# Half-swap copies of the second mixer: issued from GpSimd's queue in place of SyncE's

## Chip, cores and metric

One core of one Trainium2 chip runs the whole program. The metric is the time in microseconds (us) of one execution on the device, as the median of the timed runs. "us" and "ns" below are taken from timed runs and from one profiled execution. PE is TensorE's matmul unit, DVE VectorE, ACT ScalarE, POOL GpSimd and SP SyncE; "SPq" is the row of the instructions with which SP starts transfers.

## What is computed

The reference is a trunk of two layers over 512 positions of width 1024. Each layer has a mixer, a cross-attention into 256 memory tokens and a gated feed-forward part with a short convolution. The second layer's mixer is the one that matters here:

```
def mixer_cd(hn, w_in, w_out, ...):
    u_c, h_d = split_sizes(hn @ w_in, (C_WIDTH, 2 * D_WIDTH))
    y_f = s5_scan(u, ...)                       # a complex diagonal recurrence over the 512 positions
    y_b = flip(s5_scan(flip(u), ...))           # the same, backwards
    y = y_f + y_b + d_skip * u_c
    z = gelu(y);  o_c = z * sigmoid(z @ w_glu + b_glu)
    o_d = conformer_conv(h_d, ...)              # gate, 31-tap depthwise convolution, layernorm, silu
    return concatenate([o_c, o_d]) @ w_out
```

## The kernel before

Activations are held with channels on the 128 partitions and the 512 positions along the free dimension. Every large matmul is done three times over float32r operands that are split into a high and a low part: `wload` copies a 128x1024 block of weights to `wh` on ACT (line 201) and subtracts it to get `wl` on DVE (line 202), and `mm3` issues the three products (lines 206, 207, 208). The raw weights come from HBM into three rotating buffers `wr`, all by SP (line 147), in one fixed order; a load can start when the `wl` subtraction of three loads earlier has freed its buffer.

The second mixer runs four groups of 128 channels (i = 0 to 3). The string `CD` writes out the order of its stages; a letter and the group name each. The stages that matter:

- `c` and `C` (`c_`, lines 1365 to 1389) are the forward and the backward scan of a group. PE makes the scan's input (line 1374), ACT copies it to `t1` (tile name T, line 1377), and two transfers of 64 partitions each write `t1s` as `t1` with its upper and lower halves swapped (lines 1378 and 1379): real and imaginary parts sit on the two halves. DVE then multiplies `t1` in place by a table (line 1380), multiplies `t1s` (1381), adds (1382), scans (1384 or 1386), and multiplies the scan's result twice (1387, 1388). Line 1380 overwrites `t1`, so it waits for both transfers.
- `s` (`s_`, lines 1391 to 1396) swaps the halves of both results of a group into `xs` (tile X2s), again by two transfers for each direction; they wait for line 1388.
- `x` (line 1402) adds on DVE what `s` brought to what line 1387 left; `y` (lines 1416 and 1418) multiplies the sum on PE.
- `q` is two of the 31 taps of the convolution, each one instruction on DVE (line 1463); 'u', 'v' and 'g' are blocks of the input projection, 'k' steps of the keys and values of the next cross-attention, 'w' and 'Z' load and apply convolution tables for PE.
- `l`, `L`, `m` load tables for the scans (tiles bm, cst, cm) from scratch in HBM, all by SP. The tile cst has two buffers: the load for a group waits until line 1388 of the group before has read its old contents.

So SP's queue holds three kinds of work in one order: half-swap copies, table loads and weight loads. SP waits for the inputs of the instruction at its head before it goes on. A planner orders each engine's instructions by its own estimate of when they can run; `pinned` fixes, for the engines that it is given, that the first instruction of a stage stays behind the last one traced before it. In this mixer these are PE and SP (`PS_`, line 1536), DVE for `q`. GpSimd's only use of its own queue for transfers is line 793, in the first mixer, which loads four tiles of the input (256 KB each, 128 partitions).

Of the kernel before, what the change touches and what calls it, by code (L numbers as in the profile page):

```python
# [90 lines left out]
def trunk(ctx, tc, xT, memT, pos, vec, amask, cmask, bmask,  # L91
          w_z, w_ab, w_abv, w_oab, w_xq, w_xk, w_xv, w_xo, w_up, w_dn, wg2,
          w_cd, w_glu, w_ocd, s5v, s5b, s5bs, s5c, s5cs, ctab, out, upto=99):
    nc = tc.nc
    V, A, G, PE = nc.vector, nc.scalar, nc.gpsimd, nc.tensor
# [7 lines left out]
    def nm(p):  # L103
        n_[0] += 1
        return f"{p}_{n_[0]}"
# [32 lines left out]
    def tp_ps():  # L138
        return PS.tile([128, 512], F32, tag="tp", bufs=2, name=nm("tp"))
# [1118 lines left out]
    def mixer_cd(norm, nnext, kv):  # L1258
# [3 lines left out]
        def b2(tag, bufs):  # L1262
            return T.tile([128, S], F32, tag=tag, bufs=bufs, name=nm(tag))
# [20 lines left out]
        def half0(j):  # L1284
            if j in part:
                return
            H, L = wload(None, 1024, wnext(srcs, WAHEAD), G if j in LPOOL else V)
            part[j] = mm_ps(), H, L
            half1(j, 0)
            if j == first:  # L1290
                half1(j)
# [73 lines left out]
        def c_(i, d):  # L1365
            BM, cst = tab[i, d], rot[i, d]
            ct, st, rt = cst[:, 0], cst[:, 1], P.tile([128, S], F32, tag="nsq", bufs=2, name=nm("rt"))
            A.activation(g3(rt), rho[:, 32 * d + 8 * i:32 * d + 8 * i + 8].unsqueeze(2).to_broadcast([128, 8, 64]),
                         AF.Copy)
            V.memset(g3(rt)[:, :, 63 * d:63 * d + 1], 0.0)  # L1370
            fl = (lambda v: g3(v)) if d == 0 else (lambda v: g3(v)[:, :, ::-1])
            tp = tp_ps()
            for g in range(8):
                PE.matmul(tp[:, 64 * g:64 * g + 64], BM[:, 128 * g:128 * g + 128], Rg[i][:, 64 * g:64 * g + 64],
                          start=True, stop=True)
            t1, t1s = b2("T1", 3), b2("T1s", 2)
            A.activation(t1, tp, AF.Copy)
            nc.sync.dma_start(t1s[0:64], t1[64:128])
            nc.sync.dma_start(t1s[64:128], t1[0:64])
            V.tensor_tensor(g3(t1), g3(t1), fl(ct), ALU.mult)  # L1380
            V.tensor_tensor(g3(t1s), g3(t1s), fl(st), ALU.mult)
            V.tensor_tensor(t1, t1, t1s, ALU.add)
            if d == 0:
                V.tensor_tensor_scan(t1s, rt, t1, 0.0, op0=ALU.mult, op1=ALU.add)
            else:
                V.tensor_tensor_scan(t1s[:, ::-1], rt[:, ::-1], t1[:, ::-1], 0.0, op0=ALU.mult, op1=ALU.add)
            V.tensor_tensor(g3(t1), g3(t1s), fl(ct), ALU.mult)
            V.tensor_tensor(g3(t1s), g3(t1s), fl(st), ALU.mult)
            X[i, d] = t1, t1s

        def s_(i):
            for d in range(2):
                xs, t1s = b2("X2s", 2), X[i, d][1]
                nc.sync.dma_start(xs[0:64], t1s[64:128])
                nc.sync.dma_start(xs[64:128], t1s[0:64])
                X[i, d] = X[i, d][0], xs

        def x_(i):
# [130 lines left out]
        def k_(i):  # L1529
            for _ in range(min(i, len(ksteps))):  # L1530
                if ksteps[0] == kv.norm:
# [1 line left out]
                ksteps.pop(0)()  # L1533
                tabset("gelu_apprx_tanh_and_others", True)

        PS_ = (PE, nc.sync)
        stage = {"u": (PS_, u_), "a": (PS_, a_), "b": (PS_, b_), "x": ((), x_), "y": (PS_, y_),
                 "l": (PS_, l_), "L": (PS_, r_), "m": (PS_, m_), "s": (PS_, s_),
                 "c": (PS_, lambda i: c_(i, 0)), "C": (PS_, lambda i: c_(i, 1)),
                 "f": (PS_, f_), "v": (PS_, lambda i: half0(4 + i)), "V": (PS_, v_),  # L1540
                 "g": (PS_, lambda i: half0(8 + i)), "G": (PS_, g_),
                 "A": (PS_, ca_), "B": (PS_, cb_), "w": (PS_, w_), "Z": (PS_, z_), "q": ((V,), q_), "F": (PS_, cf_), "N": (PS_, n_),
                 "k": (PS_, k_), "K": (PS_, lambda i: kv.load())}
# [79 lines left out]
    eskv = ExitStack()  # L1623
    kv1 = KV(1, eskv)
    mixer_cd(n3, n4, kv1)
    if upto == 3:
        return dump()
# [106 lines left out]
```

## Time and profile before

| | us |
|---|---|
| median of 3 runs | 1602.35 |
| lowest and highest | 1599.77, 1603.43 |
| the profiled execution, as timed | 1605.85 |
| its span, first to last instruction | 1604.1 |
| PE busy in the span | 1558.4 (97%) |
| DVE, ACT, POOL busy | 1072.0, 707.6, 327.3 |

The second mixer's scans lie between about 884 and 1008 us of the span. A row of the timeline gives start, duration, engine, line, tiles and, in brackets, how long the engine was idle just before and what ended that. A row of SPq is the issue of a transfer, not the transfer. In a table of stretches each engine's busy time stands with its count of instructions, then the granted TensorE clock as a share of 2.4 GHz, the DMA engines' busy share and the rate in GB/s.

### The profile page before, as it was taken

The page shows a single profiled execution, that of the slowest core. Times are in us where ns is not written, and L with a number is a line of the kernel's source. Part 1 is how long each engine was busy: PE and PEld are TensorE (multiplying, and loading weights), DVE is VectorE, ACT ScalarE, POOL GpSimd, SP SyncE. Part 2 cuts the span into 40 slices and gives each one's busy share as a digit, 9 for nine tenths or more (in the row PEclk, how much of TensorE's full clock was granted, in tenths as well). Part 3 has the DMA queues.
Part 4 walks back from the last instruction along what each step waited for, and adds up shares of the span by engine and source line. Part 5 has one row for each costly group of instructions (what it writes and reads, how often), then busy time and mean ns, then how long its engine had stood idle before and what let it go on. Part 6 is the DMA issues. An engine that isn't in the chain of part 4 may idle for free.

```text
span 1604.1 us, 20956 instructions
## 1 busy us (share of the span) xinstructions
PE 1558.4 (97%) x8036; PEld 1303.9 (81%) x8036; DVE 1072.0 (67%) x1492; ACT 707.6 (44%) x1089; POOL 327.3 (20%) x354
## 2 busy tenths in 40 slices
PE   9999999999999998998999998999999999999997
PEld 6787889888888776786788877888888888888887
DVE  7586766467568789479846797476646766636644
ACT  5464755355444344233336343374535444424423
POOL 8402000000049953553520000000000111100101
PEclk9999999999999999999999999999999999999998
DMA  5323333231222334544545666453202232332331
GB/s 179 109 65 94 110 114 106 79 118 57 76 73 94 120 116 122 168 125 128 149 151 202 210 223 224 157 184 107 90 27 92 94 103 93 96 101 92 95 104 65
DMA packets 76117, 189.11 MB, mean 118 GB/s; under 512 B 8368, under 2 KB 27440, under 8 KB 76016
## 3 DMA queue, kind: packets, MB, share of 16 engines
q1 hardware_dynamic: 75376, 186.58, 36.1%
q8 instruction: 63, 1.03, 0.3%
q0 software_dynamic: 320, 1.05, 0.2%
q14 instruction: 38, 0.31, 0.1%
q10 hardware_dynamic: 320, 0.13, 0.0%
HBM read 162.43 MB, written 19.01 MB: 113 GB/s over the span
## 4 chain that ended last, share of the span: by engine, by line
PE 70%; DVE 13%; POOL 6%; DMA 4%; ACT 3%; issue 3%; SPq 1%; ACTq 0%; DVEq 0%; POOLq 0%
PE mm L206 20%; PE mm L208 20%; PE mm L207 20%; DVE wl L202 2%; PE mm L737 2%; PE sc L1489 1%; DVE t L972 1%; DMA T1s<-T 1%; DVE t L971 1%; PE tp L724 1%; DVE t L976 1%; POOL t L1139 1%; PE sc L208 1%; PE sc L206 1%; PE sc L207 1%
## 5 line engine op out<-in xcount | busy, mean ns | idle before, releaser
L201 ACT ACTIVATE wh<-wr 128x1024 fp32r<-128x1024 f32 (+1 forms) x229 | 239.0, 1045 | 428.4 <-PE mm L207 311.3
L208 PE MATMUL mm<-hg,wl 128*128 128x512 f32 x1000 | 392.9, 393 | 15.9 <-DVE wl L202 15.9
L206 PE MATMUL mm<-hg,wh 128*128 128x512 f32 x1000 | 396.9, 397 | 1.3 <-ACT wh L201 1.3
L207 PE MATMUL mm<-hg,wh 128*128 128x512 f32 x1000 | 391.3, 391 | 0.0
L202 DVE TENSOR_TENSOR wl<-wr,wh 128x1024 fp32r<-128x1024 f32 (+1 forms) x229 | 296.2, 1294 | 76.4 <-ACT wh L201 74.4
L208 PEld LDWEIGHTS mm<-hg,wl 128*128 128x128 f32 x1000 | 189.0, 189 | 60.3 <-DVE wl L202 19.8
L206 PEld LDWEIGHTS mm<-hg,wh 128*128 128x128 f32 x1000 | 189.2, 189 | 42.9 <-issue 2.2
L207 PEld LDWEIGHTS mm<-hg,wh 128*128 128x128 f32 x1000 | 189.1, 189 | 39.5 <-issue 1.2
L976 POOL TENSOR_TENSOR t<-t,t 128x512 f32<-128x512 f32 x22 | 28.9, 1315 | 626.7 <-ACT t L182 622.7
L208 PE MATMUL mm<-g,wl 128*128 128x512 f32 x324 | 126.7, 391 | 2.7 <-DVE wl L202 2.7
L206 PE MATMUL mm<-g,wh 128*128 128x512 f32 x324 | 126.9, 392 | 0.0
L207 PE MATMUL mm<-g,wh 128*128 128x512 f32 x324 | 126.2, 389 | 0.0
L968 DVE TENSOR_TENSOR u<-mm,R 128x512 f32<-128x512 f32 x88 | 60.3, 687 | 74.2 <-PE mm L208 74.0
L970 ACT ACTIVATE t<-u,vt 128x512 f32<-128x512 f32 x88 | 70.8, 806 | 50.3 <-DVE u L968 50.2
L986 DVE TENSOR_TENSOR h<-mm,h 128x512 f32<-128x512 f32 x40 | 27.6, 691 | 87.8 <-PE mm L208 87.7
L972 DVE SCALAR_TENSOR_TENSOR t<-u,vt,t 128x511 f32<-128x511 f32 x88 | 78.5, 892 | 4.3 <-DMA dct<-tr 1.8
L971 DVE SCALAR_TENSOR_TENSOR t<-u,vt,t 128x511 f32<-128x511 f32 x88 | 75.4, 857 | 8.0 <-ACT t L970 8.0
L208 PEld LDWEIGHTS mm<-g,wl 128*128 128x128 f32 x324 | 60.8, 188 | 16.4 <-DVE wl L202 3.5
L182 ACT ACTIVATE t<-t 128x512 f32<-128x512 f32 x44 | 27.8, 633 | 104.2 <-DVE t L972 104.2
L207 PEld LDWEIGHTS mm<-g,wh 128*128 128x128 f32 x324 | 60.8, 188 | 12.6
L206 PEld LDWEIGHTS mm<-g,wh 128*128 128x128 f32 x324 | 60.9, 188 | 12.2
L279 DVE TENSOR_TENSOR h<-mm,h 128x512 f32<-128x512 f32 x32 | 21.7, 688 | 46.2 <-PE mm L208 46.2
(520 smaller groups left out, 2981.7 us busy)
## 6 DMA issues: line engine op xcount, KB each, us to landing
wr<-in_w_up SPq DMA_DIRECT2D x88, 512.0 KB
wr<-in_w_dn SPq DMA_DIRECT2D x32, 448.0 KB
wr<-in_w_ab SPq DMA_DIRECT2D x16, 512.0 KB
wr<-in_w_xv SPq DMA_DIRECT2D x16, 512.0 KB
wr<-in_w_xk SPq DMA_DIRECT2D x16, 512.0 KB
wr<-in_w_xq SPq DMA_DIRECT2D x16, 512.0 KB
wr<-in_w_xo SPq DMA_DIRECT2D x16, 512.0 KB
wr<-in_w_dn SPq DMA_DIRECT2D x16, 512.0 KB
```

What stands on the lines that cost most here:

```text
L182: tabbed(A.activation(dst, src, fn, **kw))
L201: A.activation(H[:, :n], raw[:, :n], AF.Copy)
L202: (eng or V).tensor_tensor(L[:, :n], raw[:, :n], H[:, :n].bitcast(F32), ALU.subtract)
L206: PE.matmul(ps, lH, rH, start=start, stop=False)
L207: PE.matmul(ps, lH, rL, start=False, stop=False)
L208: PE.matmul(ps, lL, rH, start=False, stop=stop)
L737: PE.matmul(onat[:, 64 * j:64 * j + 64], pt[:, 128 * jt:128 * jt + 128], va[:, jt, 64 * hd:64 * hd + 64], start=jt == 0, stop=jt == 3)
L968: V.tensor_tensor(u, ps, R, ALU.mult)
L970: A.activation(t, u, AF.Identity, scale=vc(f"cw{l}", 44 + i), bias=vc(f"cb{l}", i))
L971: V.scalar_tensor_tensor(t[:, 1:], u[:, :S - 1], vc(f"cw{l}", i), t[:, 1:], op0=ALU.mult, op1=ALU.add)
L972: V.scalar_tensor_tensor(t[:, :S - 1], u[:, 1:], vc(f"cw{l}", 88 + i), t[:, :S - 1], op0=ALU.mult, op1=ALU.add)
L976: (V if l == 0 else G).tensor_tensor(res[1], res[1], res[0], ALU.mult)
```

## The change

The four lines that issue the half-swap copies call `G` (GpSimd) in place of SP, and the tuple of engines on which the mixer's stages are pinned gets G as a third. Nothing else is edited.

```
@@ c_
             A.activation(t1, tp, AF.Copy)
-            nc.sync.dma_start(t1s[0:64], t1[64:128])
-            nc.sync.dma_start(t1s[64:128], t1[0:64])
+            G.dma_start(t1s[0:64], t1[64:128])
+            G.dma_start(t1s[64:128], t1[0:64])
@@ s_
-                nc.sync.dma_start(xs[0:64], t1s[64:128])
-                nc.sync.dma_start(xs[64:128], t1s[0:64])
+                G.dma_start(xs[0:64], t1s[64:128])
+                G.dma_start(xs[64:128], t1s[0:64])
@@ mixer_cd
-        PS_ = (PE, nc.sync)
+        PS_ = (PE, nc.sync, G)
```

That is 16 pairs of copies, eight of lines 1378 and 1379 and eight of lines 1394 and 1395; each copy moves 64 partitions of 512 float32, 128 KB.

## Rows read from the trace of the kernel before

**Rows 1.** Timeline of PE, 910 to 1010 us: rows with idle before them.
```profile
919.65 1.06 PE L1336 MATMUL tp<-ident,uT 128*64 128x128 f32 x8 [1.02 <-DVE uT L1327]
...
965.88 0.79 PE L207 MATMUL mm<-wl,mg 128*128 128x512 f32 x1 [2.45 <-DVE wl L202]
971.69 0.50 PE L206 MATMUL mm<-hg,wh 128*128 128x512 f32 x1 [1.11 <-ACT wh L201]
972.95 0.50 PE L208 MATMUL mm<-hg,wl 128*128 128x512 f32 x1 [0.53 <-DVE wl L202]
...
1003.12 0.70 PE L207 MATMUL mm<-wl,mg 128*128 128x512 f32 x1 [1.83 <-DVE wl L202]
```

**Rows 2.** Table of stretches: PE, PEld, DVE, ACT, POOL, clock, DMA share, GB/s.
```profile
964.00:969.00 5.00, 3.12 (x7) 2.48 (x8) 5.00 (x9) 0.00 (x0) 0.00 (x0) 0.67 1.02 306
...
1080.00:1250.00 170.00, 170.00 (x808) 142.20 (x807) 104.66 (x158) 79.25 (x135) 0.00 (x0) 1.00 0.25 81
```

**Rows 3.** Timeline of DVE, 884 to 1020 us.
```profile
892.93 0.69 DVE L1380 TENSOR_TENSOR T<-T,cst 128x512 f32<-128x512 f32 x1 [3.34 <-DMA T1s<-T]
...
906.63 0.69 DVE L1402 TENSOR_TENSOR xp<-T,X2s 128x512 f32<-128x512 f32 x1 [0.52 <-DMA X2s<-T1s]
...
914.01 0.69 DVE L1380 TENSOR_TENSOR T<-T,cst 128x512 f32<-128x512 f32 x1 [1.85 <-DMA T1s<-T]
...
943.79 0.69 DVE L1380 TENSOR_TENSOR T<-T,cst 128x512 f32<-128x512 f32 x1 [0.23 <-DMA T1s<-T]
...
962.70 0.69 DVE L1402 TENSOR_TENSOR xp<-T,X2s 128x512 f32<-128x512 f32 x1
...
964.61 1.22 DVE L202 TENSOR_TENSOR wl<-wr,wh 128x1024 fp32r<-128x1024 f32 x1
965.74 0.68 DVE L1402 TENSOR_TENSOR xp<-T,X2s 128x512 f32<-128x512 f32 x1
...
971.67 1.23 DVE L202 TENSOR_TENSOR wl<-wr,wh 128x1024 fp32r<-128x1024 f32 x1 [1.31 <-ACT wh L201]
...
991.95 0.69 DVE L1380 TENSOR_TENSOR T<-T,cst 128x512 f32<-128x512 f32 x1 [1.63 <-DMA T1s<-T]
```

**Rows 4.** Timeline of SP's issues, 850 to 1090 us.
```profile
889.85 0.54 SPq L1378 DMA_DIRECT2D T1s<-T  x1
...
907.35 0.47 SPq L1378 DMA_DIRECT2D T1s<-T  x1
...
939.03 0.47 SPq L1378 DMA_DIRECT2D T1s<-T  x1
...
958.82 0.47 SPq L1394 DMA_DIRECT2D X2s<-T1s  x1
...
962.09 0.46 SPq L1394 DMA_DIRECT2D X2s<-T1s  x1
...
963.23 1.27 SPq L1363 DMA_DIRECT2D cst<-dct  x2
964.60 0.38 SPq L147 DMA_DIRECT2D wr<-in_w_cd  x1
...
987.11 0.46 SPq L1378 DMA_DIRECT2D T1s<-T  x1
```

**Rows 5.** Waits of SP's queue, 850 to 1090 us: total us, times, longest.
```profile
SPq L1378 <- ACT T L1377: 38.8, 5, 18.1
...
SPq L1394 <- DVE rt L1370: 20.0, 2, 13.4
```

**Rows 6.** Line 793, transfers issued by POOL: durations of the issue, landing (all four; one at 286.3).
```profile
L793 POOL DMA_DIRECT2D h<-in_xT x4: 536/542/743, 260.1 to 288.8; - x4
...
DMA to landing us min/median/max: 2.7/3.5/4.5
...
DMA to landing us min/median/max: 4.1/4.1/4.1
```

**Rows 7.** Table of stretches, the one around POOL's issue at 286.3.
```profile
284.00:288.00 4.00, 4.00 (x33) 3.65 (x31) 2.90 (x8) 3.30 (x8) 0.54 (x1) 1.00 0.87 265
```

## The prediction

> **What bounds the kernel now.** I read the idle time of PE in the mixer's stretch first, then who ended it, then the engine behind that. After the mixer PE is never idle (170.00 of 170.00 us at full clock [rows 2]), so whatever PE gets back in the mixer stays until the end, and a gap of PE is the only place where time can be won or lost. PE's timeline shows few gaps. Four carry the sum: 2.45, 1.11, 0.53 and 1.83 us, all for a block of weights that ACT or DVE had not yet split; one of 1.02 us at 919.65 only matters on the way [rows 1]. Three of the four wait for DVE's subtraction `wl`, so the next view is DVE's timeline. At 964 to 969 DVE is busy in 5.00 of 5.00 us while PE has 3.12 [rows 2]: here the order of work on DVE decides. DVE's own idle time before that lies at the half-swap copies: 0.52 us for X2s and 1.85 and 0.23 us for T1s, later 1.63 us more [rows 3]. The 3.34 us at 892.93 are the first pair's, when there is nothing else on DVE to do.
>
> Last, SP's issues and waits. SP stood 38.8 us at line 1378 and 20.0 us at line 1394 waiting for inputs of copies, up to 18.1 us at a time [rows 5], and all loads traced behind them stood too. Much of this is harmless, since PE's gaps are only those above.
>
> I write P for the time from the first issue of a pair to the DVE instruction that waited for it. From the issue to line 1380, SP's pairs took 892.93 - 889.85 = 3.08 us on quiet DMA engines, then 914.01 - 907.35 = 6.66, 943.79 - 939.03 = 4.76 and 991.95 - 987.11 = 4.84 us with loads in the queue [rows 3, 4].
>
> **What the change does, part by part.** Sixteen pairs leave SP and go to POOL. POOL computes nothing in this stretch (0.00 us in 964 to 969, and so in the rest of the scans [rows 2]), so its waits for ACT and DVE stop nothing but the next pair, and the pairs come in the order in which their inputs become ready. The added pin on G costs no instruction.
>
> *POOL's P.* The trace of before has four transfers that POOL issued: 0.54 us an issue, landing 2.7 to 4.5 us after it [rows 6]. They are 256 KB from HBM, and mine 128 KB within SBUF. The one at 286.3 met loads in flight (DMA share 0.87, 265 GB/s [rows 7]) and took 4.1 us. At 265 GB/s 128 KB less is 0.5 us less. An estimate for a loaded pair is thus 0.54 for the first issue, plus 4.1, less 0.5, which is about 4.2 us; for a quiet one 0.54 + 2.7 - 0.5 = 2.7 us. Bounds: 2.7 us, and 6.7 us, SP's own worst under load. I take 4.2 with loads and, at the first pair, no difference from SP's 3.08.
>
> The page "DMA: Bandwidth & Descriptors" of the Trainium skill (section "Queues, rings and completion order") says that each DMA engine takes turns packet by packet between the queues that have work; by that a copy in a queue of its own need not wait for megabytes of loads ahead of it, as SP's 6.66 us pair did. The 4.1 us at share 0.87 agree with it, but it is one transfer.
>
> *Step 1, group 1.* The pair issued at 907.35 lands at 907.35 + 4.2 = 911.55. Without the 0.52 and 1.85 us waits DVE would come to line 1380 at 914.01 - 2.37 = 911.64, so it no longer waits, and DVE's work behind it moves up by 2.4 us. At P = 6.7 the gain is 0.
>
> *Step 2, group 2.* The pair at 939.03 follows PE, and PE moves up only by its 1.02 us gap at 919.65. It is issued at 938.0 and lands at 942.2, against 943.79: DVE is now 1.6 us ahead, not 2.4 us.
>
> *Step 3, copies behind the scans of group 2.* SP's X2s were in time: 962.70 - 958.82 = 3.88 us and 965.74 - 962.09 = 3.65 us passed before the additions, and neither waited [rows 3, 4]. At 4.2 us the first is 0.3 us late. The subtraction at 964.61, for which PE's 2.45 us gap waits, stands behind it, so this gap shrinks by 1.6 - 0.3 = 1.3 us. The second copy is issued by 1.6 us earlier, at 960.5, and lands at 964.7, where DVE arrives at 965.74 - 1.3 = 964.4: another 0.3 us. DVE is 1.0 us ahead.
>
> *Step 4, the weight load behind them.* The load of `wr` at 964.60 stood on SP behind two copies for each direction and the cst loads [rows 4]. The cst loads wait for the same line 1388, so SP isn't free of that wait, but two issues (0.46 and about 0.6 us, from 962.09 to 963.23) go from in front of the load, and 0.5 MB of copies from its queue; the first cst load no longer stands behind the second pair either. With DVE's 1.0 to 1.6 us the load goes out at about 961, 3 to 4 us earlier. DVE then finds `wh` ready and loses its 1.31 us wait at 971.67. The subtraction starts 1.0 + 1.3 = 2.3 us earlier, and so does PE's matmul at 972.95. (This contains the 1.3 us of step 3.)
>
> *Step 5, group 3.* The last pair's 4.84 us become 4.2: DVE is 0.6 us earlier at 991.95, and has no idle between that and the `wl` that ends PE's 1.83 us gap at 1003.12. At P = 2.7 the gap goes altogether, at 6.7 it grows by 1.9. Loads that SP now starts early (it stood 18.1 us ahead of this group) are then in flight or done; I keep the loaded value.
>
> *The sum:* 2.3 + 0.6 = 2.9 us off the profiled execution, 1605.85 to 1602.95. The timed median stands 3.5 us below that execution, so I take the same 2.9 us off it: **1599.4 us**. The loads that SP starts earlier have no price apart from step 4: PE's other gaps don't wait for them.
>
> **The rivals.**
> - *A larger gain.* The mean granted clock fell to 0.67 in 964 to 969, part of it at the lower level of 1.2 GHz, behind the idle time around 966 [rows 1, 2]; that costs 5 x 0.33 = 1.65 us. If pairs take 3.1 us even with loads (SP's quiet value), steps 1 to 3 give 2.4 us without loss, step 4 then 3.7, step 5 the whole 1.7; with the clock's 1.65 that is some 7 us: 1595.3. For it: the loads queued by SP may be done before the copies come. Against: share 1.02 at 964 to 969.
> - *Slower: the copies don't overtake.* The Trainium skill, the same page, section "Issuing engines are not separate DMA queues", says that transfers of all issuers run on the same 16 engines and interleave, and that another issuer saves only issue time. As a mechanism here: on saturated engines POOL's pair takes what SP's took, 6.7 us. Then group 1 gains nothing; group 2 loses 6.7 - 4.76 = 1.9; the first X2s is 6.7 - 3.88 = 2.8 us late and delays `wl` at 964.61 to 4.7 us later, the second is late by about 0.2 more; step 4 gives back 1.3; group 3 loses 1.9. That is 4.9 - 1.3 + 1.9 = 5.5 us slower: 1607.9. The sum is nil at P of about 5.4 and 3.2 us slower at about 6.1. For it: 1.02 of DMA share. Against: the 4.1 us of POOL's row.
> - *Nothing.* DVE's shift is spent where an engine waits in order for another (the 5.92 us of four gaps shrink in one place and open in the next), or the planner, whose estimate of POOL's transfers I don't see, writes another order on DVE that takes the gain: 1602. The order can also go either way by as much as a gap, about 2.5 us.
>
> **How the numbers follow.** My forecast's case has 0.48, with its own range of 1597 to 1602 (P from 3.5 to 5). The larger gain has 0.18, the copies that don't overtake 0.18, nothing 0.16. A measurement of this kernel tells about 0.2%, 3.2 us, from no change. The forecast's 2.9 us lies just under that: of its 0.48 I put 0.23 on faster, 0.24 on the same and 0.01 on slower. The larger gain is faster. Of the third, 0.15 is slower and 0.03 the same. Of the last, 0.03 is faster, 0.10 the same, 0.03 slower. Together faster 0.44, same 0.37, slower 0.19. The range of 8 in 10 goes from 1594.5, taking in the larger gain, to 1606, most of the way to the third.
>
> **What would show it.** Right: the 1.85 and 0.52 us before lines 1380 and 1402 gone; P at about 4.2 on POOL in groups 1 to 3; the gaps at 966 and 972 shorter by together over 2 us; `wr` issued some 3 us earlier against DVE's line 1388; SP's waits at 1378 and 1394 gone, with waits for `wl` and for PE in their place. Wrong: DVE idle at line 1402 in group 2 by more than 1 us, P over 5 us, or another order of lines 202, 1402 and 1463 on DVE around the gaps. If P is as I say and PE's gaps are not shorter, the chain from DVE's waits to PE's gaps was misread.

## The result: slower, 1.1%

The changed kernel took 1619.87 us in the median (1618.05 to 1624.52), the kernel before 1601.06 us (1597.09 to 1603.43) beside it: a ratio of 1.0107, 95% interval 1.0082 to 1.0133, some 17 us by the ratio. Forecast were 1599.4 us and a range that ended at 1606. The profiled execution has a span of 1616.3 us, 12.2 more than before's 1604.1; it came to the first pair of copies 4.2 us earlier in its span (885.61 in place of 889.85 [rows 4]), so its loss from there on is 16.4 us. From the first pair's issue to the last gap of PE in the mixer it needed 1014.15 - 885.61 = 128.5 us, before 1003.12 - 889.85 = 113.3 [rows 1, 4]: 15 of the 16.4 us are lost inside the mixer.

PE's timeline of the changed kernel, all rows from 900 to 1030 us with idle before them (the counterpart of [rows 1]):

```profile
915.01 1.86 PE L1418 MATMUL sc<-cm,xp 128*64 128x128 f32 x6 [5.77 <-issue]
943.70 0.49 PE L206 MATMUL mm<-wh,mg 128*128 128x512 f32 x1 [0.66 <-ACT wh L201]
944.96 0.80 PE L207 MATMUL mm<-wl,mg 128*128 128x512 f32 x1 [0.77 <-DVE wl L202]
968.78 0.73 PE L206 MATMUL mm<-wh,mg 128*128 128x512 f32 x2 [1.19 <-ACT wh L201]
970.35 0.50 PE L207 MATMUL mm<-wl,mg 128*128 128x512 f32 x1 [0.83 <-DVE wl L202]
979.56 0.80 PE L206 MATMUL mm<-hg,wh 128*128 128x512 f32 x1 [6.02 <-ACT wh L201]
1014.15 0.80 PE L207 MATMUL mm<-wl,mg 128*128 128x512 f32 x1 [2.63 <-DVE wl L202]
```

Two gaps of 6 us are new. The one at 979.56 waits for weights that ACT had not rounded; the one at 915.01, where the profile names no releaser, ends 0.78 us after DVE began the addition `xp` at 914.23, whose result this matmul reads. Who kept ACT and DVE? First DVE's timeline (against [rows 3]), then ACT's:

```profile
891.37 0.69 DVE L1380 TENSOR_TENSOR T<-T,cst 128x512 f32<-128x512 f32 x1 [6.29 <-DMA T1s<-T]
...
913.09 1.23 DVE L202 TENSOR_TENSOR wl<-wr,wh 128x1024 fp32r<-128x1024 f32 x1 [5.35 <-ACT wh L201]
914.23 0.68 DVE L1402 TENSOR_TENSOR xp<-T,X2s 128x512 f32<-128x512 f32 x1
...
979.54 1.22 DVE L202 TENSOR_TENSOR wl<-wr,wh 128x1024 fp32r<-128x1024 f32 x1 [5.32 <-ACT wh L201]
```

```profile
912.00 2.19 ACT L201 ACTIVATE wh<-wr 128x1024 fp32r<-128x1024 f32 x2 [5.61 <-DMA wr<-in_w_xv]
...
978.46 1.06 ACT L201 ACTIVATE wh<-wr 128x1024 fp32r<-128x1024 f32 x1 [9.24 <-DMA wr<-in_w_cd]
```

Both long gaps end when a load of weights has landed. The first has another cause beside it, the order on DVE. In the kernel before both additions `xp` stood ahead of this `wl`:

```profile
907.89 0.69 DVE L1402 TENSOR_TENSOR xp<-T,X2s 128x512 f32<-128x512 f32 x1
...
915.22 1.22 DVE L202 TENSOR_TENSOR wl<-wr,wh 128x1024 fp32r<-128x1024 f32 x1
```

In the changed kernel the planner put `wl` first, and DVE stood idle 5.35 us for its weights, although the pair that the first `xp` needs had landed at about 909.3 (the later copy's issue at 902.46 and 6.8 us to its landing). The load itself was little slower than before: from issue to ACT's use 912.77 - 904.43 = 8.3 us before, 912.00 - 902.70 = 9.3 now.

SP's and POOL's issues show where the loads stood (SP's queue first, against [rows 4]; then POOL's):

```profile
884.71 2.11 SPq L1358 DMA_DIRECT2D bm<-dbm  x2
901.69 0.92 SPq L1363 DMA_DIRECT2D cst<-dct  x2
902.70 0.38 SPq L147 DMA_DIRECT2D wr<-in_w_xv  x1
...
967.21 0.93 SPq L1363 DMA_DIRECT2D cst<-dct  x2
968.23 0.38 SPq L147 DMA_DIRECT2D wr<-in_w_cd  x1
```

```profile
885.61 0.60 POOL L1378 DMA_DIRECT2D T1s<-T  x1 [26.58 <-ACT T L1377]
...
901.96 0.52 POOL L1394 DMA_DIRECT2D X2s<-T1s  x1 [13.53 <-DVE T1s L1388]
...
967.47 0.52 POOL L1394 DMA_DIRECT2D X2s<-T1s  x1 [21.00 <-DVE T1s L1388]
...
968.49 0.52 POOL L1394 DMA_DIRECT2D X2s<-T1s  x1
```

In SP's own queue the copies had gone out before the loads traced behind them. Now a load goes out just ahead of several pairs: `bm` 0.90 us before the first T1s pair, `cst` 0.27 us before X2s at 901.96, and 0.26 us before X2s at 967.47; the last two because POOL and SP wait for the same instruction of DVE and SP issued first. Copies and loads then share the DMA engines (DMA share 1.04 and 1.03 from 905 to 910 and 910 to 915 us): the first pair's P is 891.37 - 885.61 = 5.76 us, and the load at 968.23 is used by ACT at 978.46, 10.2 us after its issue, where before 970.58 - 964.60 = 6.0 us passed (ACT's next use of that load began at 970.58; the issue is in [rows 4]). Landings of POOL's copies, from the answers on lines 1378 and 1394 (us from issue to landing: least, median, most, of eight each):

```profile
L1378 POOL DMA_DIRECT2D T1s<-T x8: 516/518/596, 885.6 to 997.6; - x8
DMA to landing us min/median/max: 3.0/5.3/5.8
...
L1394 POOL DMA_DIRECT2D X2s<-T1s x8: 516/516/523, 902.0 to 1012.0; - x8
DMA to landing us min/median/max: 2.3/4.8/9.0
```

The gaps cost twice, by the clock behind them (table of stretches, columns as in [rows 2]):

```profile
915.00:920.00 5.00, 4.87 (x22) 4.51 (x23) 4.93 (x8) 0.54 (x1) 1.03 (x2) 0.50 0.65 198
945.00:950.00 5.00, 5.00 (x22) 3.88 (x23) 4.93 (x8) 1.65 (x3) 1.47 (x3) 0.67 1.02 345
...
980.00:985.00 5.00, 4.96 (x12) 3.38 (x12) 4.93 (x8) 2.21 (x4) 0.00 (x0) 0.50 0.61 218
985.00:990.00 5.00, 5.00 (x29) 4.09 (x28) 3.64 (x5) 1.06 (x1) 0.00 (x0) 0.91 0.00 0
...
1015.00:1020.00 5.00, 5.00 (x19) 3.77 (x19) 5.00 (x8) 2.02 (x4) 0.00 (x0) 0.50 0.00 0
```

Behind the gaps of 5.77, 6.02 and 2.63 us PE ran 5 us at the lower level, 1.2 GHz: three times 2.5 us. The other two rows cost 1.65 and 0.45, and the stretch from 920 to 925 us, at 0.90, another 0.5: 10.1 together. Before, the stretch of [rows 2] cost 1.65 and the two from 1000 to 1010 us, at 0.82 and 0.83, another 1.75. That is some 7 us more. The gaps themselves grew from 8.5 us (6.9 of them in [rows 1]) to 17.9, by 9.4. Together these are about the loss of 16.4 us.

### The profile page after: what moved, and what is told of

It is laid out like the page before. It is cut to its first block, busy times and chain, and to the rows that moved or that the text cites. A ratio compares the mean times of both kernels' runs of the same rounds, so it can differ in the third digit from the quotient of the medians.

```text
span 1616.3 us, 20971 instructions
## 1 busy us (share of the span) xinstructions
PE 1564.7 (97%) x8036; PEld 1309.8 (81%) x8036; DVE 1069.9 (66%) x1492; ACT 707.4 (44%) x1089; POOL 346.8 (21%) x386
## 3 DMA queue, kind: packets, MB, share of 16 engines
q8 instruction: 63, 1.03, 0.3%
## 4 chain that ended last, share of the span: by engine, by line
PE 73%; DVE 12%; POOL 6%; ACT 3%; DMA 3%; issue 3%; SPq 1%; DVEq 0%; ACTq 0%; POOLq 0%
PE mm L206 21%; PE mm L208 21%; PE mm L207 20%; DVE wl L202 2%; PE mm L737 2%; PE sc L1489 1%; DVE t L971 1%; DVE t L972 1%; PE tp L724 1%; DMA T1s<-T 1%; DMA wr<-in_w_cd 1%; POOL t L1139 1%; PE sc L1418 1%; PE sc L208 1%; PE sc L207 1%
## 5 line engine op out<-in xcount | busy, mean ns | idle before, releaser
L207 PEld LDWEIGHTS mm<-g,wh 128*128 128x128 f32 x324 | 60.9, 188 | 12.5
```

Source lines behind the costliest of these rows:

```text
L207: PE.matmul(ps, lH, rL, start=False, stop=False)
```

## The experiments

Three theories. **Loads:** the copies have lost their place ahead of SP's loads, and a load issued just before or beside them is served first. **GpSimd:** copies issued from POOL are slow in themselves. **Order:** the planner, with other estimates for the copies, wrote another order for PE, DVE and ACT (`wl` ahead of `xp` above is one place), and this order is what costs. For the runs marked "old order" the order of PE, DVE, ACT and SP in the mixer was written out as the kernel before has it, by a chain of dependences without semaphores:

```diff
-    ffn(1, n5, None)
+    ffn(1, n5, None); fix_order(nc, tc)
...
+    for text in ORDER.values():
+        names = [f"I-{n}" for n in _numbers(text)]
+        for p, q in zip(names, names[1:]):
+            tc.add_manual_dep(by[q], p, mybir.DependencyInfo(
+                mybir.DependencyClass.NoSync, mybir.DependencyReason.DATA), reason="order written out")
```

The first four runs stand beside 1602.99 us of the kernel before.

**1. All copies on POOL, old order** (the change and the lines above).

> The changed kernel with the order of PE, DVE, ACT and SP in the second mixer written out as it was before; only the copies are on POOL. The changed kernel is about 18 us (1.1%) slower than before. Theory O (the planner's other order on DVE and PE is the cost): this stands within 4 us of before. Theory L (SP's loads are no longer held back by the copies' waits and now share the DMA engines with the copies): 12 to 18 us slower, as the changed kernel. Theory Q (a copy on POOL's queue lands later whatever SP does): 8 to 18 us slower.

1620.49 us, ratio 1.0106 (1.0085 to 1.0127): as slow as the change. The order isn't needed for the loss. With DVE in its old order it waits for the copies themselves; before it waited 0.52 us for X2s in all [rows 3]. DVE's waits from 884 to 1030 us (total, times, longest):

```profile
DVE T L1380 <- DMA T1s<-T: 17.0, 3, 10.5
DVE xp L1402 <- DMA X2s<-T1s: 12.5, 5, 3.5
```

**2. As 1, SP held for the copies' inputs.** SP's next load behind each group of copies waits for what the copies wait for (lines 1377 and 1388), as when the copies stood in its queue.

```diff
+    for load, wait in HELD:
+        tc.add_manual_dep(by[f"I-{load}"], f"I-{wait}", mybir.DependencyInfo(
+            mybir.DependencyClass.Sync, mybir.DependencyReason.DATA), reason="load held back as before")
```

> As e1, and in addition each load of SP that followed a copy before waits for what that copy waited for (line 1377 or 1388). Theory L: within 4 us of before. Theory Q: the pairs still take 5 to 9 us under load, and the kernel is 5 to 15 us slower. Theory O: as e1, within 4 us.

1624.33 us, ratio 1.0128 (1.0107 to 1.0149). That seems to speak against the loads, but they weren't held as meant. SP's, POOL's and DVE's rows of the first two pairs:

```profile
898.14 0.33 SPq L1408 DMA_DIRECT2D cm<-dmt  x1
```

```profile
896.62 0.60 POOL L1378 DMA_DIRECT2D T1s<-T  x1 [26.54 <-ACT T L1377]
...
898.41 0.52 POOL L1378 DMA_DIRECT2D T1s<-T  x1 [0.67 <-ACT T L1377]
```

```profile
899.59 0.69 DVE L1380 TENSOR_TENSOR T<-T,cst 128x512 f32<-128x512 f32 x1 [3.51 <-DMA T1s<-T]
905.48 0.69 DVE L1380 TENSOR_TENSOR T<-T,cst 128x512 f32<-128x512 f32 x1 [3.87 <-DMA T1s<-T]
```

The first pair took 2.97 us, less than SP's 3.08: so POOL is not slow in itself. The second took 7.07: SP's load had gone out 0.27 us before it. The wait that was to hold the loads let SP in first, by 0.26 to 0.27 us, at the second pair in six of the eight groups of copies.

**3. Copies on SP, but VectorE and TensorE in the changed kernel's order.** The kernel before with the chain above, the lists taken from the changed kernel:

```diff
-    ffn(1, n5, None)
+    ffn(1, n5, None); fix_order(nc, tc)
```

> The kernel before, copies on SP, with the order of DVE and PE in the second mixer written out as the planner made it for the changed kernel. Theory O: 8 to 18 us slower than before, PE's gaps near 910 and 975 us are there. Theories L and Q: within 4 us of before, since SP holds the loads back and the copies go ahead of them.

1621.59 us, ratio 1.0121 (1.0083 to 1.0159). The new order is bad by itself too. PE's two longest gaps:

```profile
926.10 0.62 PE L1418 MATMUL sc<-cm,xp 128*64 128x128 f32 x4 [3.74 <-issue]
...
995.47 0.79 PE L206 MATMUL mm<-hg,wh 128*128 128x512 f32 x1 [5.07 <-ACT wh L201]
```

They stand at the same two instructions as the changed kernel's long gaps (5.77 and 6.02 us), and at the first DVE again has `wl` (924.17, after 4.77 us of idle time for its weights) ahead of `xp` (925.31). Run 1 has 1.02 us at the first place and nothing at the second; its long gaps are elsewhere. So in the changed kernel the order sets where PE stands, and at these two places the copies' new queue adds about 2.0 and 1.0 us, as far as two traces compare. Either part alone costs what both together cost; they don't add up.

**4. Only the X2s copies on POOL, old order.**

```diff
-                nc.sync.dma_start(xs[0:64], t1s[64:128])
-                nc.sync.dma_start(xs[64:128], t1s[0:64])
+                G.dma_start(xs[0:64], t1s[64:128])
+                G.dma_start(xs[64:128], t1s[0:64])
```

> Only the copies behind the scans (lines 1394 and 1395) on POOL, the others on SP, order of PE, DVE, ACT and SP as before. Theories L and Q: most of the cost, 6 to 14 us slower, since these copies were in front of the cst and weight loads on SP. Theory O: within 4 us of before.

1616.88 us, ratio 1.0089 (1.0064 to 1.0114); L1402 waited 12.4 us for X2s, in six waits. Moved alone, the pairs behind the scans cost 14 us, where all pairs cost 17.

The next four stand beside 1604.38 us.

**5. As 1, SP held until the copies have landed.**

```diff
+    for load, copies in HELD:
+        for wait in copies:
+            tc.add_manual_dep(by[f"I-{load}"], f"I-{wait}", mybir.DependencyInfo(
+                mybir.DependencyClass.Sync, mybir.DependencyReason.DATA), reason="load behind the copies' landing")
```

> Copies on GpSimd's queue as in the changed kernel, the other engines' instructions in the order of the kernel before, and SyncE starts its next load behind each group of copies only when that group has landed. Arrival order (a load issued just before or beside the copies is served first, and the copies on a queue of their own have lost their place ahead of it): with no load under way the copies land about as in the quiet window, 2.3 to 3 us after their issue in place of 5 to 9, the waits of L1402 for X2s come down from 12.5 us to 4 or less, and the kernel is at 1602 to 1609 us. GpSimd's copies slow in themselves: they still land 5 us or more after their issue, and the kernel stays at 1615 us or above, or above that by what the late loads cost.

1614.14 us, ratio 1.0062 (1.0037 to 1.0088). Missed on the time, right on the landings that the trace shows: with no load under way pairs took 2.97 (888.79 to 891.76), at most 3.12, 3.59 and 3.38 us, and L1402's waits fell to 1.5. The pair at 907.18 still took 7.08: the loads held for the pairs before it started at 907.40, beside it. And loads that wait for landings come late: PE's gaps of 2.52 and 2.45 us near 970 are for weights again.

**6 and 7. Only the T1s copies moved, old order, to ScalarE's queue (6, the diff) and to GpSimd's (7, with G for A).**

```diff
-            nc.sync.dma_start(t1s[0:64], t1[64:128])
-            nc.sync.dma_start(t1s[64:128], t1[0:64])
+            A.dma_start(t1s[0:64], t1[64:128])
+            A.dma_start(t1s[64:128], t1[0:64])
```

> The T1s copies (ahead of the scans) are issued from ScalarE's queue, the X2s copies (behind the scans) stay on SyncE's, the other engines' order is that of the kernel before. Arrival order: they too stand on a queue of their own beside SyncE's loads, so they land about as late as GpSimd's, 4 to 7 us, L1380's waits come to some 17 us (before about 8), and the kernel is 3 to 10 us slower than before, as with the T1s copies on GpSimd's queue. GpSimd's queue slow in itself: ScalarE's copies land within 3 us and the kernel is within 2 us of the one before, while the run with GpSimd isn't.

> The T1s copies alone are issued from GpSimd's queue, X2s stay on SyncE's, the order of the other engines is that of the kernel before. All copies moved cost +17 us in this order and the X2s copies alone +14, so if the two parts add up this run is +3 us (1606); if each part alone is enough to put the second mixer's chain out of step it is +10 us or more (1613). L1380's waits should stand near the 17 us of the run with all copies moved, L1402's near those of the kernel before.

ScalarE: 1614.54 us, ratio 1.0057 (1.0032 to 1.0083). GpSimd: 1613.31 us, ratio 1.0048 (1.0028 to 1.0068). The two are alike also in the first pair, with `bm` issued 0.63 and 0.89 us ahead of it: P is 907.33 - 900.96 = 6.37 and 895.39 - 889.26 = 6.13 us. The theory GpSimd has fallen: ScalarE's queue does the same.

**8. The kernel before with the cm loads of two tiles earlier in the stage list.**

```diff
-... b0 k1 u1 c0 C0 m0 q0 k1 ...
+... b0 k1 u1 m0 c0 C0 q0 k1 ...
-... q1 k1 s1 q0 f0 L2 q1 v2 m1 q0 ...
+... q1 k1 m1 s1 q0 f0 L2 q1 v2 q0 ...
```

> The kernel before, copies on SyncE, with two stages of loads in the stage list put earlier: the cm loads of tile 0 ahead of c0, those of tile 1 ahead of s1, so that they run while the DMA engines have little to do, and not ahead of the weight loads behind the copies. If the weights' landing ends the gaps of TensorE near 965 and 972 us, they shrink and the kernel is 1 to 4 us faster (1599 to 1602). If the planner's order, which changes with the list, weighs more than any load (as in the run with the copies on SyncE in the changed kernel's order, +18.6 us), the time can go either way by 5 us or more.

1601.81 us, ratio 0.9998 (0.9975 to 1.0022): no difference. PE's gaps near 960 and 963 are still 2.27 and 2.25 us, and wait for `wh` and `wl` as before.

**9. The pair by itself beside loads.** Nothing of the computation is left; VectorE's memsets let loads and a pair go at chosen times:

```diff
+    def loads(q, n):
+        for k in range(n):
+            keep(V.memset(ld[k][:, 0:1], 0.0), "V")
+        for k in range(n):
+            keep(ENG[q].dma_start(ld[k], w_cd[k]), q)
+
+    def pair(q):
+        keep(V.memset(t1, 1.0), "V")
+        keep(ENG[q].dma_start(t1s[0:64], t1[64:128]), q)
+        keep(ENG[q].dma_start(t1s[64:128], t1[0:64]), q)
```

> No part of the computation is left in this kernel: it times the pair of half-swap copies (two of 128 KB) by itself, from SyncE's, ScalarE's and GpSimd's queue, with 0, 1, 2, 4 or 6 loads of 512 KB issued some 1 us ahead of it or just behind it. P is the time from the pair's first issue to the VectorE instruction that needs both. Arrival order, whatever the queue: P is about 3 us with no load, grows by up to 1.3 us (512 KB at some 400 GB/s) with each load ahead, to 6 to 8 us at four loads, for all three queues alike, and loads issued behind the pair add less than 1 us. Equal shares between queues: a pair on a queue of its own stays at 3 to 4.5 us with any number of loads, ahead or behind, and only the pair on the loads' own queue comes to 6 to 8. GpSimd's queue slow in itself: its P is 1 us or more above that of the other two at every number of loads, at none too.

P in us, the two repetitions of each. In the loads' own queue all "ahead" loads have gone out before the pair. From another queue the first goes out 0.55 us before the pair (0.8 before POOL's) and the others follow every 0.4 us, so only two are ahead of it and the rest beside it.

```
loads of 512 KB        SP's queue    ACT's queue   POOL's queue
none                   2.98, 2.97    2.96, 2.99    2.99, 2.83
1 ahead                4.53, 3.90    4.07, 4.26    3.79, 3.75
2 ahead                5.44, 5.64    5.82, 6.11    5.56, 5.61
4 ahead                8.30, 8.66    8.00, 7.97    8.32, 7.70
6 ahead                9.79, 9.62    7.72, 7.80    7.95, 8.99
4 behind               2.98, 2.94    5.16, 5.05    5.32, 5.34
```

With the loads moved to ACT's queue, a pair in SP's took 7.78 and 7.63 us with four ahead, 5.07 and 5.21 with four behind. Rows of the lines "4 ahead" and "4 behind" for POOL, and of "4 behind" for SP: SP's queue, POOL, and DVE's instruction that needs the pair.

```profile
103.40 1.75 SPq L126 DMA_DIRECT2D ld<-in_w_cd  x4
...
164.50 0.47 SPq L130 DMA_DIRECT2D t1s<-t  x1
...
165.70 26.77 SPq L126 DMA_DIRECT2D ld<-in_w_cd  x12
...
190.69 1.79 SPq L126 DMA_DIRECT2D ld<-in_w_cd  x4
```

```profile
104.24 0.52 POOL L130 DMA_DIRECT2D t1s<-t  x1 [35.03 <-DVE t L129]
...
190.40 0.52 POOL L130 DMA_DIRECT2D t1s<-t  x1 [40.16 <-DVE t L129]
```

```profile
112.56 0.69 DVE L142 TENSOR_TENSOR t1s<-t1s,t 128x512 f32<-128x512 f32 x1 [8.62 <-DMA t1s<-t]
...
167.48 0.69 DVE L142 TENSOR_TENSOR t1s<-t1s,t 128x512 f32<-128x512 f32 x1 [2.43 <-DMA t1s<-t]
...
195.72 0.69 DVE L142 TENSOR_TENSOR t1s<-t1s,t 128x512 f32<-128x512 f32 x1 [5.04 <-DMA t1s<-t]
```

All queues are alike with no load, and all wait alike for loads ahead: one load lands 1.25 us after another here, and 4 loads add 4.7 to 5.7 us to P. The difference is behind the pair: in the loads' own queue four loads behind it add nothing, from another queue they add 2.1 to 2.5 us. That the shared queue itself shields the pair isn't shown, since the loads also start later there: SP issues both copies first, and its first load leaves 165.70 - 164.50 = 1.20 us after the pair's first issue. From another queue it leaves 0.29 us after POOL's first issue and 0.55 us after ACT's or SP's. In run 11 below loads leave another queue 1.17 us after POOL's pair, and the pair isn't delayed. So the time between pair and load is enough to explain every row with loads behind; a shared queue gives that time by its order of issue. A shared queue with loads closer behind was not tried. Moving the copies thus frees them of nothing that is ahead and lets loads leave beside them. My expectation "loads behind add less than 1 us" holds only for those that leave some 1.2 us behind the pair.

The Trainium skill, page "DMA: Bandwidth & Descriptors", section "Queues, rings and completion order", says that an engine takes turns between queues packet by packet. An estimate by that, if the turns are alike in bytes, which no run shows: 256 KB take 0.6 us at the loads' pace and 1.2 us in equal turns, so P would be some 3.6 us with any number of loads. Here a pair in a queue of its own took 3.8 to 4.3 us with one load ahead and 7.7 to 8.3 with four; the measurement decides.

**10 and 11. As 1, SP held until the copies have been issued.** A memset on POOL behind each group of copies, and SP's next load waits for it. In run 10 it writes a new tile of 4 bytes a partition, in run 11 a padding tile that was there already.

```diff
             G.dma_start(t1s[64:128], t1[0:64])
+            if d == 1:
+                G.memset(flag, 0.0)
...
+    for load, flag in HELD:
...
+        tc.add_manual_dep(by[f"I-{load}"], f"I-{flag}", mybir.DependencyInfo(
+            mybir.DependencyClass.Sync, mybir.DependencyReason.DATA), reason="load behind the copies' issue")
```

> Copies on GpSimd's queue, all engines in the order of the kernel before, and a small memset on GpSimd behind each group of copies: SyncE starts its next load when that memset is done, so just after the copies have been issued, as when they stood in its own queue. Arrival order: the copies have their place ahead of the loads back, the first two pairs come to 3 to 3.5 us each (in the run that held the loads only for the copies' inputs the second took 7.07), the waits of L1402 for X2s fall from 12.5 to under 4 us, and the kernel is within 5 us of the one before, 1600 to 1608 us. If order of issue is not what decides: the pairs stay at 5 to 7 us beside the loads and the kernel at 1615 us or above.

> As the run before it, but the memset behind each group of copies writes into the padding tile that is there already, in place of a new tile. In the run before it the mixer's stretch from the first pair's issue to TensorE's last gap took 113.1 us (113.3 in the kernel before), but each matmul on hg behind the mixer took 395 to 396 ns in place of 389, some 7 us in all. If the new tile, which moved hg in SBUF, did that, they are at 389 again, and the kernel is within 3 us of the one before (1601 to 1607 us beside 1604): with the loads behind the copies' issue nothing of the change's cost is left, which is what order of issue claims. If the matmuls stay at 395, or the mixer is 5 us or more longer than before, something else of GpSimd's queue costs, and the kernel stays at 1610 us or above.

Run 10: 1614.73 us beside 1604.84, ratio 1.0060 (1.0029 to 1.0092), a miss that had nothing to do with the copies. Its mixer took 113.1 us (890.59 to 1003.68), but behind it the matmuls on `hg` were slower than before and in every other run; groups of PE from 1250 to 1500 us, run 10, then run 11 (busy, mean ns):

```profile
L206 PE MATMUL mm<-hg,wh 128*128 128x512 f32 x295 | 116.7, 396 | 0.0
```

```profile
L206 PE MATMUL mm<-hg,wh 128*128 128x512 f32 x304 | 118.3, 389 | 0.0
```

Run 11: **1604.64 us beside 1604.73, ratio 0.9989 (0.9965 to 1.0013)**. The whole loss is gone, with every copy still on GpSimd's queue. The second pair and the load behind it (SP, POOL, and DVE's line 1380, which is 1382 here):

```profile
893.10 0.33 SPq L1411 DMA_DIRECT2D cm<-dmt  x1
```

```profile
891.93 0.52 POOL L1378 DMA_DIRECT2D T1s<-T  x1 [0.67 <-ACT T L1377]
892.44 0.52 POOL L1379 DMA_DIRECT2D T1s<-T  x1
892.95 0.12 POOL L1381 MEMSET pad<- 128x1 f32 x1
```

```profile
895.05 0.69 DVE L1382 TENSOR_TENSOR T<-T,cst 128x512 f32<-128x512 f32 x1
```

The load now goes out 1.17 us after the pair in place of 0.27 us before it (run 2), and the pair is there within 3.12 us, without a wait, in place of 7.07. The medians from issue to landing of the pairs' first copies are 3.6 us for T1s and 2.9 for X2s, in run 1 4.6 and 5.3. Runs 2 and 11 differ in what SP waits for, and so in this order; it is worth some 22 us (1.0128 against 0.9989). DVE had no wait for X2s left.

**12. As 11, the planner left to order the engines.**

```diff
-    for text in ORDER.values():
-        names = [f"I-{n}" for n in _numbers(text)]
...
     for load, flag in HELD:
```

> The same waits of the loads behind the copies' issue, but the planner is left to order the engines itself. If order of issue alone decides, this is within 4 us of the kernel before too. If the planner's order with the copies on GpSimd's queue costs of itself (the copies on SyncE in the changed kernel's order of VectorE and TensorE were 18.6 us slower), the kernel is 6 us or more above the run with the order written out.

1608.77 us beside 1604.73, ratio 1.0022 (1.0001 to 1.0043), some 4 us above run 11, between the two expectations: the planner's order costs something here too, about a quarter of the change's loss. Its profile has a gap of 4.08 us where the changed kernel has 6.02. It isn't the changed kernel's order, though: here `xp` (911.43) stands ahead of `wl` (921.78) on DVE again. The changed kernel's own order with the loads held was not run.

No version beats the kernel before; run 11 and run 8 equal it.

## Why the prediction was wrong

- **What bounds the kernel: right.** What PE loses in the mixer it never gets back; 15 of 16.4 us are in the mixer. That SP's long waits at lines 1378 and 1394 were "harmless" was wrong in the other sense: they were useful. They kept up to seven loads behind a group of copies.
- **POOL's P: wrong, the first step that failed.** 4.2 us under load rested on one transfer of line 793 [rows 6, 7], issued at 286.34. SP's last load had gone out at 283.90, and the next only after 310 us, so nothing stood beside it or close ahead. Measured: 5.76 at the first pair, where "no difference from SP's 3.08" had been taken; a pair's first copy landed 5.3 us (T1s) and 4.8 us (X2s) after its issue in the median, 9.0 at the most. For quiet engines the estimate of 2.7 was fair (2.83 to 2.99, and 2.3 for one copy). The price is not POOL's; it is that of loads at the copies' side, which the change itself brought there.
- **"The loads that SP starts earlier have no price apart from step 4": wrong, one of the two roots.** Their price is P of the pairs, and their own landing: in the old order all of the loss, 17 us (run 1), which is gone when the loads leave behind the copies (run 11). The text saw that SP would be free and booked it as a gain only.
- **The planner's order, left out of the sum: the other root.** It stood only among the rivals, at up to 2.5 us; by itself it cost 18.6 us (run 3). Line 202 ahead of line 1402 on DVE, behind the gap of 5.77 us, is one of the signs of being wrong that the prediction had listed.
- **Step 1: half right.** The 1.85 us wait at line 1380 in group 1 is gone. In its place DVE waits 5.35 us for the weights of the load at 902.70, used 9.3 us after its issue, with `xp` standing behind them in the new order.
- **Steps 2 and 3: not reached.** The X2s pair of group 2 was forecast 0.3 us late; its copies landed 4.8 to 9.3 us after their issue. In the old order (run 1) DVE waited 12.5 us for X2s in all.
- **Step 4: wrong in sign.** The load of `wr` did go out earlier, 0.26 us before the second pair's issue in place of 2.5 us after it (964.60 - 962.09 [rows 4]). It landed later, 10.2 us after its issue in place of 6.0, and PE's gap of 1.11 us became one of 6.02. With the new order and the copies on SP it is 5.07 (run 3).
- **Step 5: wrong.** The last gap grew from 1.83 to 2.63 us.
- **The rivals.** "The copies don't overtake" was the right mechanism for the copies. It cited the Trainium skill, page "DMA: Bandwidth & Descriptors", section "Issuing engines are not separate DMA queues", for transfers that interleave whoever issued them. Run 9 agrees: 2.83 to 2.99 us with no load and 7.7 to 8.7 with four ahead, from all three queues. The rival's 5.5 us were too few for four reasons: it delayed only copies, not the weights beside them; it took SP's worst P as the ceiling, though in SP's queue no load leaves close behind a pair (1.20 us in run 9) and now loads leave beside it; it left out the clock, about 7 us here; and it kept the old order.
- **What stays open.** How the 17 us of the change itself divide between the loads and the new order can't be said: each alone costs as much (runs 1 and 3), and its two long gaps are those of run 3. Why a load in SP's queue takes 10 us beside 0.5 MB of copies and 1 MB ahead of it was not taken apart.

## What to carry to other kernels

A queue is also an order: a small copy that stands in the loads' own queue goes out ahead of the loads behind it, and its wait for its input holds them back. Before such a copy is moved to another queue, list what the old queue will issue while the copy waits; if those loads then leave in the same microsecond, the copy pays for their megabytes and the loads for the copy. If it must move, let the old queue's next load wait until the copy has been issued, not until its input is ready. And where a planner orders the engines by its own estimates, compare its order before and after: here the new order alone cost as much as the loads.

## What the hardware showed unexpectedly

- With a new tile of 4 bytes a partition the matmuls on `hg` took 395 to 396 ns in the mean in place of 389, about 7 us in all; with the memset in an existing tile they are at 389 (runs 10 and 11). That it moved `hg` to another place in SBUF is the likely reason; addresses were not read.
- A wait on the same event lets SP issue 0.26 to 0.27 us before POOL, which was enough to put a load ahead of the copies (the changed kernel and run 2).
- Four loads from another queue that start 0.3 to 0.6 us after a pair delay it by 2.1 to 2.5 us (run 9). Loads that start 1.2 us after it don't, be it from its own queue (2.94 and 2.98 us, run 9) or another (at most 3.12 us, run 11).
- A gap of 6.02 us left PE at 1.2 GHz for the following 5 us (clock 0.50 from 980 to 985).
